# A two-layer streaming encoder trunk: the scale of the attention scores moves into the queries, and the softmax maximum is written negated

## The chip, the cores and the metric

One Trainium2 chip, one of its cores. The metric is the device time of one execution in microseconds (us). Engines are called by the profile's names: PE (TensorE, matmuls; its weight loads are listed apart as PEld), DVE (VectorE), ACT (ScalarE), POOL (GpSimd) and SP (SyncE, which issues most DMAs). L551 means line 551 of the kernel before.

## The reference

Two layers over 512 frames of width 2048, all in float32. Each layer normalises h, projects it through one wide matrix, and feeds the columns to three attention mixers: A (6 heads, low-rank queries and keys, width 128 + 64 rotary), B (5 heads; an indexer picks 128 keys of each query), and C (5 heads, each the difference of two softmaxes over width 64). Every branch has a SiLU gate. An output projection, a residual and a gated per-layer embedding follow. The scale is 192, 128 or 64 to the power -1/2 (A, B, C).

```python
sc = jnp.einsum('bqhd,bkhd->bhqk', qb, k) * scale
pr = masked_softmax(sc, chunk_mask(blk, s)).astype(v.dtype)
return jnp.einsum('bhqk,bkhd->bqhd', pr, v)
...
a1 = masked_softmax(jnp.einsum('bqhd,bkhd->bhqk', qb[..., 0, :], k1) * scale, mask)
a2 = masked_softmax(jnp.einsum('bqhd,bkhd->bhqk', qb[..., 1, :], k2) * scale, mask)
pr = (a1 - lam * a2).astype(v.dtype)
```

## The kernel before

Float32 products are made of three PE matmuls: every operand is split into a rounded part `hi` (by ACT) and a rest `lo` (by DVE), and `mm3` (L361) adds hi·hi, hi·lo and lo·hi in PSUM. Where both parts of a 64-row operand fit on 128 partitions, `stack` (L266) puts hi on one half and lo on the other, and `mm2` needs two matmuls. `split_into` (L260), `stack`, `twice` (L276) and `split` (L286) make these parts.

A layer runs 15 groups of the input projection (192 matmuls each, one of them 96), then 4 groups of `w_o` and 4 of `w_pg`. Each group accumulates four PSUM tiles called `pp`, over 8 chunks of weights (`wr`, split into `wh` and `wl` at L352 to L357). When a group ends, its four `pp` tiles must be read out before the next group can write the same four banks: by ACT at L636 (a copy to `z`), or for gate columns by DVE at L911 (a product with R) and a SiLU by ACT at L912.

The attention runs as a side stream: after every three projection matmuls `pump` (L405) lets the generator `mixers` issue a piece. In order: the six heads of A (heads 0 to 5), the indexer, the five of C (heads 6 to 10), the five of B (heads 11 to 15); a second stream, `choose` (L780), picks the keys for B by 16 rounds of DVE's MAX and MATCH_REPLACE. For each head and each of 4 query blocks, the scores go to a PSUM tile `at`, `causal` masks it (L558), and `soft` (L547) does the softmax: the row's maximum (L550, DVE), its product with -scale (L551, DVE), exp with that bias and with the scale, and its row sum (L552, ACT), and a reciprocal (L553, DVE). The probabilities `e` are normalised, `attend` (L560) transposes them on PE (L568), splits them into `th` and `tl` (L261, L262) and multiplies with v (at L363 to L365, `at<-th,g`). Then ACT copies the head's output away (L828 and L647 for C, L647 else), and the queries and keys of the next head are rotated on DVE (L538 to L541) and split.

At the end of a layer the gated outputs are split once more (`mix`, L934) and are the moving operand of `w_o`; the first four of them lie in tiles called `z`.

The order of instructions on each engine is not the order of the Python code. The program is built under

```python
with tile.TileContext(nc, schedule_with_timeline_sim=True) as tc:
```

so a scheduler at build time arranges the queues by a model of time of its own. Each engine then runs its queue strictly in that order; a removed instruction can therefore shift what stands next to what in all queues.

Of the kernel before, what the change touches and what calls it, by code (L numbers as in the profile page):

```python
# [15 lines left out]
AF = mybir.ActivationFunctionType  # L16
ALU = mybir.AluOpType
AX = mybir.AxisListType
# [10 lines left out]
SC_A = 192 ** -0.5  # L29
SC_B = 128 ** -0.5  # L30
SC_C = 64 ** -0.5
# [167 lines left out]
def trunk(ctx: ExitStack, tc: tile.TileContext, t, out):  # L199
    nc = tc.nc  # L200
    PE, ACT, DVE, POOL = nc.tensor, nc.scalar, nc.vector, nc.gpsimd
# [9 lines left out]
    def f32(ap):  # L211
        return ap.bitcast(F32)

    def slot(dt=F32):
        return big.tile([128, 512], dt, name="g", tag="g")

    def tmp():
        return work.tile([128, 512], F32, name="t", tag="t", bufs=N_TMP)
# [7 lines left out]
    def at():  # L226
        return psum.tile([128, 512], F32, name="at", tag="at")
# [4 lines left out]
    def sm(n=1):  # L232
        return small.tile([128, 4], F32, name="sm", tag="sm", bufs=16)[:, :n]
# [23 lines left out]
    onesf = const.tile([128, 2], F32, name="onesf")  # L257
    DVE.memset(onesf, 1.0)

    def split_into(hi, lo, src):  # L260
        ACT.activation(hi, src, AF.Copy)  # L261
        DVE.tensor_tensor(lo, src, f32(hi), op=ALU.subtract)  # L262

    TOP, LOW = slice(0, 64), slice(64, 128)

    def stack(y):  # L266

        res = []
        for a, b in ((TOP, LOW), (LOW, TOP)):
            o = slot(F32R)  # L270
            ACT.activation(o[a], y[a], AF.Copy)
            DVE.tensor_tensor(o[b], y[a], f32(o[a]), op=ALU.subtract)
            res.append(o)
        return res

# [7 lines left out]
        DVE.tensor_tensor(lo[b], y[a], f32(hi[a]), op=ALU.subtract)  # L283
        return hi, lo

    def split(src):  # L286
        n = src.shape[1]
        hi, lo = slot(F32R)[:, :n], slot(F32R)[:, :n]
        split_into(hi, lo, src)
        return hi, lo  # L290


# [242 lines left out]
    def rope(src, cs, rows=slice(0, 128)):  # L535

        a, b = tmp(), tmp()
        DVE.stream_shuffle(b[rows], src[rows], SWAP)  # L538
        DVE.tensor_tensor(a[rows], src[rows], cs[0][rows], op=ALU.mult)
        DVE.tensor_tensor(b[rows], b[rows], cs[1][rows], op=ALU.mult)  # L540
        DVE.tensor_tensor(a[rows], a[rows], b[rows], op=ALU.add)  # L541
        return a
# [1 line left out]
    BO = [128 * (i * (i + 1) // 2) for i in range(NB)]  # L544
    KO = [0, 512, 896, 1152]

    def soft(ps, n, scale, e):  # L547

        st = sm(4)
        DVE.tensor_reduce(st[:, 0:1], ps[:, :n], op=ALU.max, axis=AX.X)  # L550
        DVE.tensor_scalar(st[:, 1:2], st[:, 0:1], -scale, None, op0=ALU.mult)  # L551
        ACT.activation(e, ps[:, :n], AF.Exp, bias=st[:, 1:2], scale=scale, accum_out=st[:, 2:3])  # L552
        DVE.reciprocal(st[:, 3:4], st[:, 2:3])  # L553
        return st[:, 3:4]

# [33 lines left out]
    for L in range(DEPTH):  # L589
# [5 lines left out]
        tabA = (cosA, sinA)  # L595
        tab = {}
# [14 lines left out]
        raw = {}  # L611
# [73 lines left out]
        def mla():  # L685
            cq, ckv = [], []
            yield ("cq", 2)
            yield from latents("cq", 3, 384, cq)
            yield ("krki", 0)
            yield from shared_keys()  # L690
            yield ("ckv", 1)
            yield from latents("ckv", 2, 256, ckv)
            yield GAP
            kr = keys["r"]
            for j in range(3):
                g = [cc[:, CC_QG + 3 * L + k:CC_QG + 3 * L + k + 1] for k in range(3)]
                w = chunk("w_uq", L, S_UQ, 2 * j, g[:2]) + chunk("w_uq", L, S_UQ, 2 * j + 1, g[2:])
                q = []
                for m in range(3):
                    ps = at()  # L700
                    for k in range(3):
                        mm3(ps, cut(w[k], slice(128 * m, 128 * m + 128)), cq[k], k == 0, k == 2)
                    q.append(split(ps) if m < 2 else stack(rope(ps, tabA)))
                    yield 1.95
                g = [cc[:, CC_KVG + 2 * L + k:CC_KVG + 2 * L + k + 1] for k in range(2)]

                def nope_key(w):
                    ps = at()
                    for k in range(2):
                        mm3(ps, cut(w[k], slice(0, 128)), ckv[k], k == 0, k == 1)  # L710
                    return split(ps)

                w = chunk("w_ukv", L, S_UKV, 2 * j, g)
                kn = nope_key(w)
                yield 1.3
                vp = []
                for b2 in range(2):
                    ps = at()
                    for b in range(2):
                        bs = slice(128 * (2 * b2 + b), 128 * (2 * b2 + b) + 128)  # L720
                        for k in range(2):
                            mm3(ps[:, 256 * b:256 * b + 256], cut(ckv[k], bs), cut(w[k], slice(128, 384)),
                                k == 0, k == 1)
                    vp.append(split(ps))
                    yield 1.3
                for x in range(2):
                    if x:
                        kn = nope_key(chunk("w_ukv", L, S_UKV, 2 * j + 1, g))
                        yield 1.3
                    yield GAP  # L730
                    probs = new_probs()
                    for i in range(NB):
                        n = 128 * (i + 1)
                        ps = at()
                        qs = slice(128 * i, 128 * i + 128)
                        mm3(ps[:, :n], cut(q[x], qs), cut(kn, slice(0, n)), True, False)
                        mm2(ps[:, :n], q[2][x], qs, kr, n, False, True)
                        causal(ps, i)
                        e = probs[:, BO[i]:BO[i] + n]
                        r = soft(ps, n, SC_A, e)  # L740
                        DVE.tensor_scalar(e, e, r, None, op0=ALU.mult)
                        yield 5 * mm_us(n)
                    yield GAP

                    def v(kb, x=x):
                        o = 256 * (kb % 2) + 128 * x
                        return cut(vp[kb // 2], slice(o, o + 128))

                    yield from attend(probs, v)
                    put_out(2 * j + x, attend.po)  # L750


        bias, score = {}, {}
# [48 lines left out]
            return [("kc", x), ("vc" if x < 4 else "v5", 0)]  # L802

        def diff_ready(x):
            q = stack(rope(raw.pop(("qc", x)), tab["c"]))
            y = rope(raw.pop(("kc", x)), tab["c"])
            return q, [twice(y, c) for c in range(2)], None, value_parts("vc", x)

        def diff_probs(x, ops, probs):
            q, k = ops[:2]  # L810
            for i in range(NB):
                n = 128 * (i + 1)
                qs = slice(128 * i, 128 * i + 128)
                e = probs[:, BO[i]:BO[i] + n]
                e2 = tmp()[:, :n]
                rr = []
                for c in range(2):
                    ps = at()
                    mm2(ps[:, :n], q[c], qs, k[c], n, True, True)
                    causal(ps, i)  # L820
                    rr.append(soft(ps, n, SC_C, (e, e2)[c]))
                DVE.tensor_scalar(e2, e2, rr[1], lam_c[:, L:L + 1], op0=ALU.mult, op1=ALU.mult)
                DVE.scalar_tensor_tensor(e, e, rr[0], e2, op0=ALU.mult, op1=ALU.subtract)
                yield 4 * mm_us(n)
# [19 lines left out]
        def dsa_ready(x):  # L844
            if x == 0:
                tab["b"] = table("b", R)
            q = split(rope(raw.pop(("qb", x)), tab["b"]))
            k = split(rope(raw.pop(("kb", x)), tab["b"]))
            return q, k, None, value_parts("vb", x)

        def dsa_probs(x, ops, probs):
            q, k = ops[:2]
            for i in range(NB):
                n = 128 * (i + 1)
                qs = slice(128 * i, 128 * i + 128)
                ps = at()
                mm3(ps[:, :n], cut(q, qs), cut(k, slice(0, n)), True, i == 0)
                if i == 0:
                    causal(ps, i)
                else:  # L860
                    PE.matmul(ps[:, :n], identb, bias[i][:, :n], start=False, stop=True)
                e = probs[:, BO[i]:BO[i] + n]
                r = soft(ps, n, SC_B, e)
                DVE.tensor_scalar(e, e, r, None, op0=ALU.mult)
                yield 3 * mm_us(n) + n * 0.000422

# [118 lines left out]
        for g in range(4):  # L985
# [8 lines left out]
            for m in range(4):  # L994
                k = 4 * g + m
                r = res[m]
# [8 lines left out]
        for g in range(4):  # L1005
# [13 lines left out]
            for m in range(4):  # L1019
                k = 4 * g + m  # L1020
                s, r = sg[m], res[m]
# [13 lines left out]
    ps = [pp() for _ in range(4)]  # L1035
# [23 lines left out]
    for half in range(2):  # L1059
        s = slice(256 * half, 256 * half + 256)  # L1060
        for c in range(8):
# [5 lines left out]
            if half == 0 and c == 1:  # L1067
                ple = []
                for m, y in enumerate(embedding(3)):
                    ple.append(slot())  # L1070
                    ACT.activation(ple[m], y, AF.Copy)
                    r = slot()
# [8 lines left out]
        for m in range(5):  # L1081
            if m == 0:
                y = acc[:, s]
            else:
                r, y = new[11 + m][:, s], sg[m - 1]
# [27 lines left out]
```

## Time and profile before

| | |
|---|---|
| median of 3 runs | 2316.86 us (2314.5 to 2317.55) |
| the profiled execution: time | 2312.61 us |
| its span, first to last instruction | 2310.8 us |
| PE busy | 2276.2 us, 98% of the span |
| DVE busy | 1414.7 us, 61% |
| ACT busy | 1056.2 us, 46% |
| mean granted PE clock | 0.997 |

The span is covered almost completely by one engine. What is left to lose or to win is therefore found in the list of the times when PE stood idle and of what ended each of them, and not in the busy shares of the others. The profiled execution is one of the quicker ones: its time is 4.25 us under the median.

### The profile page before, as it was taken

The numbers are of one execution on the slowest core, as the hardware profiler recorded it, in microseconds if no ns is written. First come the engines' busy times: TensorE is split into PE (matmuls) and PEld (weight loads), VectorE is DVE, ScalarE is ACT, GpSimd is POOL, SyncE is SP. The second block draws the span as 40 slices with busy tenths as digits, with TensorE's granted clock in tenths as the row PEclk, the third lists the DMA queues.
The fourth block names the chain that finished last, engine by engine and source line by source line (L and its number), as shares of the span: only waits on it lengthen the run. The fifth ranks groups of instructions, "written<-read, shape, count | busy, mean of one in ns | idle before, by whom it ended". The sixth has DMA issues, their size and how long they took to land.

```text
span 2310.8 us, 30164 instructions
## 1 busy us (share of the span) xinstructions
PE 2276.2 (98%) x10978; PEld 1912.9 (83%) x10988; DVE 1414.7 (61%) x3071; ACT 1056.2 (46%) x1947; POOL 114.5 (5%) x204
## 2 busy tenths in 40 slices
PE   8999999999999999999999999999999999999997
PEld 7888888888878888888888888888887887888887
DVE  7755569987777643344556555699687765333445
ACT  6444445455555532233435444445564554222444
POOL 0000000000000011000000000000000000110003
PEclk9999999999999999999999999999999999999998
DMA  6233322332324345344332333223232243553334
GB/s 201 72 95 115 112 87 87 110 100 96 96 91 141 124 141 189 121 128 141 123 100 70 99 118 112 83 94 103 91 104 93 86 164 111 177 168 133 100 101 165
DMA packets 95221, 268.34 MB, mean 116 GB/s; under 512 B 10976, under 2 KB 26848, under 8 KB 95072
## 3 DMA queue, kind: packets, MB, share of 16 engines
q1 hardware_dynamic: 81760, 223.41, 30.0%
q0 software_dynamic: 13312, 43.00, 5.3%
q8 instruction: 86, 1.41, 0.3%
q14 instruction: 63, 0.52, 0.1%
HBM read 235.96 MB, written 30.41 MB: 115 GB/s over the span
## 4 chain that ended last, share of the span: by engine, by line
PE 97%; ACT 1%; DVE 1%; issue 1%; DMA 0%; POOL 0%; SPq 0%; POOLq 0%; ACTq 0%; DVEq 0%
PE pp L363 28%; PE pp L365 27%; PE pp L364 27%; PE at L365 3%; PE at L364 3%; PE at L363 3%; PE at L568 1%; PE at L370 1%; PE at L369 1%; PE at L312 0%; PE at L333 0%; ACT wh L356 0%; DMA x<-in_x_dram 0%; ACT g L261 0%; POOL g L1051 0%
## 5 line engine op out<-in xcount | busy, mean ns | idle before, releaser
L363 PE MATMUL pp<-g,wh 128*128 128x512 f32 (+1 forms) x2432 | 938.4, 387 | 15.3 <-ACT g L261 5.9
L364 PE MATMUL pp<-g,wh 128*128 128x512 f32 (+1 forms) x2432 | 937.0, 386 | 0.0
L365 PE MATMUL pp<-g,wl 128*128 128x512 f32 (+1 forms) x2432 | 910.2, 386 | 0.0
L356 ACT ACTIVATE wh<-wr,cc 128x512 fp32r<-128x512 f32 (+3 forms) x522 | 352.2, 683 | 460.7 <-PE pp L364 310.3
L363 PEld LDWEIGHTS pp<-g,wh 128*128 128x128 f32 x2432 | 458.2, 188 | 105.1 <-ACT g L261 5.9
L364 PEld LDWEIGHTS pp<-g,wh 128*128 128x128 f32 x2432 | 457.9, 188 | 87.4
L365 PEld LDWEIGHTS pp<-g,wl 128*128 128x128 f32 x2432 | 456.2, 188 | 87.5
L357 DVE SCALAR_TENSOR_TENSOR wl<-wr,cc,wh 128x512 fp32r<-128x512 f32 (+3 forms) x522 | 360.1, 697 | 268.3 <-ACT wh L356 261.4
L353 DVE TENSOR_TENSOR wl<-wr,wh 128x512 fp32r<-128x512 f32 x288 | 199.5, 697 | 409.8 <-ACT wh L352 375.4
L352 ACT ACTIVATE wh<-wr 128x512 fp32r<-128x512 f32 x288 | 180.3, 630 | 438.9 <-PE pp L364 402.3
L365 PE MATMUL pp<-wh,g 128*128 128x512 f32 (+1 forms) x384 | 136.3, 358 | 0.0
L364 PE MATMUL pp<-wl,g 128*128 128x512 f32 (+1 forms) x384 | 136.1, 358 | 0.0
L363 PE MATMUL pp<-wh,g 128*128 128x512 f32 (+1 forms) x384 | 122.7, 362 | 0.9 <-ACT wh L356 0.8
L552 ACT ACTIVATE e<-at,sm 128x128 f32<-128x128 f32 (+3 forms) x128 | 66.8, 524 | 71.5 <-DVE sm L551 69.4
L365 PEld LDWEIGHTS pp<-wh,g 128*128 128x128 f32 x384 | 72.2, 188 | 9.6
L364 PEld LDWEIGHTS pp<-wl,g 128*128 128x128 f32 x384 | 72.3, 188 | 9.4
L363 PEld LDWEIGHTS pp<-wh,g 128*128 128x128 f32 x384 | 69.9, 188 | 10.7 <-ACT wh L356 1.3
L550 DVE TENSOR_REDUCE sm<-at 128x1 f32<-128x128 f32 (+3 forms) x168 | 77.2, 480 | 1.6
L649 POOL DMA_DIRECT2D o_d<-t x32 | 17.3, 540 | 1134.1 <-ACT t L647 1134.1
L262 DVE TENSOR_TENSOR tl<-at,th 128x512 fp32r<-128x512 f32 (+3 forms) x128 | 54.4, 482 | 28.2 <-ACT th L261 27.8
L261 ACT ACTIVATE th<-at 128x512 fp32r<-128x512 f32 (+3 forms) x128 | 45.6, 439 | 24.3 <-PE at L568 24.3
L568 PE MATMUL at<-identf,e 128*128 128x128 f32 x320 | 55.0, 274 | 0.0
(224 smaller groups left out, 2543.0 us busy)
## 6 DMA issues: line engine op xcount, KB each, us to landing
wr<-in_w_in_dram SPq DMA_DIRECT2D x207, 512.0 KB, 3.6
wr<-in_w_pg_dram SPq DMA_DIRECT2D x72, 512.0 KB, 3.7
wr<-in_w_o_dram SPq DMA_DIRECT2D x64, 512.0 KB, 3.7
o_d<-t POOLq DMA_DIRECT2D x32, 256.0 KB, 2.3
g<-o_d SPq DMA_DIRECT2D x32, 256.0 KB, 4.3
hm_d<-t POOLq DMA_DIRECT2D x32, 256.0 KB, 3.1
wr<-in_w_in_dram SPq DMA_DIRECT2D x18, 256.0 KB, 2.6
wr<-in_w_in_dram SPq DMA_DIRECT2D x16, 264.0 KB, 2.7
```

The source lines that it names most:

```text
L261: ACT.activation(hi, src, AF.Copy)
L262: DVE.tensor_tensor(lo, src, f32(hi), op=ALU.subtract)
L352: ACT.activation(hi, r, AF.Copy)
L353: DVE.tensor_tensor(lo, r, f32(hi), op=ALU.subtract)
L356: ACT.activation(hi, r, AF.Copy, scale=g)
L357: DVE.scalar_tensor_tensor(lo, r, g, f32(hi), op0=ALU.mult, op1=ALU.subtract)
L363: PE.matmul(ps, l[0], r[0], start=start, stop=False)
L364: PE.matmul(ps, l[0], r[1], start=False, stop=False)
L365: PE.matmul(ps, l[1], r[0], start=False, stop=stop)
L550: DVE.tensor_reduce(st[:, 0:1], ps[:, :n], op=ALU.max, axis=AX.X)
L552: ACT.activation(e, ps[:, :n], AF.Exp, bias=st[:, 1:2], scale=scale, accum_out=st[:, 2:3])
L568: PE.transpose(ps[:, 128 * (i - kb):128 * (i - kb) + 128], probs[:, BO[i] + 128 * kb:BO[i] + 128 * kb + 128], identf)
```

## The change

The factor `scale` leaves `soft`. It is applied where the queries are split into parts: ACT writes hi = round(scale · q), and DVE writes lo = scale · q - hi by one instruction with a scalar operand instead of a plain subtraction. `soft` then takes the maximum with `negate=True` straight into the column that the exp reads as its bias; the product with -scale is gone, 168 times in the program.

```diff
-    def split_into(hi, lo, src):
-        ACT.activation(hi, src, AF.Copy)
-        DVE.tensor_tensor(lo, src, f32(hi), op=ALU.subtract)
+    def split_into(hi, lo, src, scale=None):
+        if scale is None:
+            ACT.activation(hi, src, AF.Copy)
+            DVE.tensor_tensor(lo, src, f32(hi), op=ALU.subtract)
+        else:
+            ACT.activation(hi, src, AF.Copy, scale=scale)
+            DVE.scalar_tensor_tensor(lo, src, scale, f32(hi), op0=ALU.mult, op1=ALU.subtract)
...
-    def stack(y):
+    def stack(y, scale=1.0):
...
-            ACT.activation(o[a], y[a], AF.Copy)
-            DVE.tensor_tensor(o[b], y[a], f32(o[a]), op=ALU.subtract)
+            ACT.activation(o[a], y[a], AF.Copy, scale=scale)
+            DVE.scalar_tensor_tensor(o[b], y[a], scale, f32(o[a]), op0=ALU.mult, op1=ALU.subtract)
...
-    def soft(ps, n, scale, e):
+    def soft(ps, n, e):
...
-        DVE.tensor_reduce(st[:, 0:1], ps[:, :n], op=ALU.max, axis=AX.X)
-        DVE.tensor_scalar(st[:, 1:2], st[:, 0:1], -scale, None, op0=ALU.mult)
-        ACT.activation(e, ps[:, :n], AF.Exp, bias=st[:, 1:2], scale=scale, accum_out=st[:, 2:3])
+        DVE.tensor_reduce(st[:, 1:2], ps[:, :n], op=ALU.max, axis=AX.X, negate=True)
+        ACT.activation(e, ps[:, :n], AF.Exp, bias=st[:, 1:2], accum_out=st[:, 2:3])
...
-                    q.append(split(ps) if m < 2 else stack(rope(ps, tabA)))
+                    q.append(split(ps, SC_A) if m < 2 else stack(rope(ps, tabA), SC_A))
...
-            q = stack(rope(raw.pop(("qc", x)), tab["c"]))
+            q = stack(rope(raw.pop(("qc", x)), tab["c"]), SC_C)
...
-            q = split(rope(raw.pop(("qb", x)), tab["b"]))
+            q = split(rope(raw.pop(("qb", x)), tab["b"]), SC_B)
```

PE, ACT, POOL and SP issue as many instructions as before. DVE issues 168 fewer, and 70 of its subtractions (22 at L262, 48 at L272) take the form with a scalar. But the scheduler arranges the queues anew, in most of the stretch in which the heads run, and alike in both layers. Three places matter to the prediction. In the rows the numbers behind the names are those of buffers; line numbers of the kernel after are 1 to 4 higher up to L550 and 3 higher behind it.

Place 1: head 8 (the third of C) ends while the `pp` tiles of the group of qb0, kb0, qb1 and kb1 (5056 to 5059 before, 5000 to 5003 after) are read out. First ACT's queue, before:

```order
L636 ACTIVATE z_5510<-pp_5056 128x512
L636 ACTIVATE z_5512<-pp_5057 128x512
L356 ACTIVATE wh_5675<-wr_5673,cc_75 128x512
L261 ACTIVATE th_4537<-at_4539 128x512
L261 ACTIVATE th_4537<-at_4546 128x384
L261 ACTIVATE th_4537<-at_4552 128x256
L261 ACTIVATE th_4537<-at_4569 128x128
L356 ACTIVATE wh_5679<-wr_5673,cc_75 128x512
L828 ACTIVATE t_4657<-at_4579 128x512
L647 ACTIVATE t_4663<-at_4579 128x512
L261 ACTIVATE g_4659<-t_4657 128x512
L636 ACTIVATE z_5514<-pp_5058 128x512
```

The same stretch of ACT's queue after:

```order
L262 ACTIVATE th_4489<-at_4491 128x512
L262 ACTIVATE th_4489<-at_4498 128x384
L262 ACTIVATE th_4489<-at_4504 128x256
L639 ACTIVATE z_5446<-pp_5000 128x512
L262 ACTIVATE th_4489<-at_4521 128x128
L639 ACTIVATE z_5448<-pp_5001 128x512
L360 ACTIVATE wh_5607<-wr_5605,cc_75 128x512
L360 ACTIVATE wh_5611<-wr_5605,cc_75 128x512
L831 ACTIVATE t_4609<-at_4531 128x512
L650 ACTIVATE t_4615<-at_4531 128x512
L262 ACTIVATE g_4611<-t_4609 128x512
L639 ACTIVATE z_5450<-pp_5002 128x512
```

In both, the third `pp` tile is read out behind the three instructions that wait for the head's output. The first two are read out before the splits of the transposes before, and among them after. PE's queue from the end of the head's product, before:

```order
L365 MATMUL at_4579<-th_4537,g_4427 128x128
L365 MATMUL pp_5518<-g_141,wl_5680 128x512
L365 MATMUL pp_5519<-g_141,wl_5680 128x512
L363 MATMUL pp_5520<-g_123,wh_5524 128x512
L364 MATMUL pp_5520<-g_124,wh_5524 128x512
```

And after; behind the last row shown stand 12 more rows on 5454 and 5455, and then the first on 5456:

```order
L369 MATMUL at_4531<-th_4489,g_4387 128x128
L367 MATMUL pp_5455<-g_123,wh_5460 128x512
L368 MATMUL pp_5455<-g_124,wh_5460 128x512
L369 MATMUL pp_5455<-g_123,wl_5461 128x512
L367 MATMUL pp_5454<-g_127,wh_5464 128x512
L368 MATMUL pp_5454<-g_128,wh_5464 128x512
L369 MATMUL pp_5454<-g_127,wl_5465 128x512
L367 MATMUL pp_5455<-g_127,wh_5464 128x512
L368 MATMUL pp_5455<-g_128,wh_5464 128x512
L369 MATMUL pp_5455<-g_127,wl_5465 128x512
```

Before, two matmuls stand between the head's product and the first that needs the third bank (5520); after, 21 stand there (5456).

Place 2: head 11 (the first of B). PE's queue around the last transpose of its probabilities, before:

```order
L365 MATMUL pp_6472<-g_141,wl_6625 128x512
L363 MATMUL pp_6473<-g_141,wh_6624 128x512
L364 MATMUL pp_6473<-g_142,wh_6624 128x512
L365 MATMUL pp_6473<-g_141,wl_6625 128x512
L568 MATMUL at_5666<-identf_88,e_5575 128x128
L363 MATMUL at_5686<-th_5640,g_5562 128x512
L364 MATMUL at_5686<-tl_5641,g_5562 128x512
```

And after:

```order
L571 MATMUL at_5598<-identf_88,e_5511 128x128
L368 MATMUL pp_6397<-g_138,wh_6540 128x512
L369 MATMUL pp_6397<-g_137,wl_6541 128x512
L367 MATMUL pp_6396<-g_141,wh_6544 128x512
L368 MATMUL pp_6396<-g_142,wh_6544 128x512
L369 MATMUL pp_6396<-g_141,wl_6545 128x512
L367 MATMUL pp_6397<-g_141,wh_6544 128x512
L368 MATMUL pp_6397<-g_142,wh_6544 128x512
L369 MATMUL pp_6397<-g_141,wl_6545 128x512
L367 MATMUL at_5618<-th_5572,g_5498 128x512
```

Eight projection matmuls have moved between the last transpose and the product with v. In both, the next row behind the product's 12 matmuls is the first on a `pp` tile that DVE's L911 must have read out.

Place 3: the end of layer 0, DVE's queue from the third to the fourth `z` rest that `w_o` needs, before:

```order
L262 TENSOR_TENSOR z_7537<-g_5043,z_7536 128x512
L262 TENSOR_TENSOR g_7545<-g_6043,g_7544 128x512
L921 TENSOR_TENSOR g_7501<-g_7501,z_7498 128x512
L262 TENSOR_TENSOR g_7561<-g_6049,g_7560 128x512
L262 TENSOR_TENSOR g_7587<-g_6451,g_7586 128x512
L262 TENSOR_TENSOR z_7541<-g_5049,z_7540 128x512
```

And after:

```order
L263 TENSOR_TENSOR z_7453<-g_4987,z_7452 128x512
L924 TENSOR_TENSOR g_7411<-g_7411,z_7408 128x512
L263 TENSOR_TENSOR g_7561<-g_6799,g_7560 128x512
L924 TENSOR_TENSOR g_7417<-g_7417,z_7414 128x512
L263 TENSOR_TENSOR g_7587<-g_7097,g_7586 128x512
L263 TENSOR_TENSOR g_7603<-g_7109,g_7602 128x512
L263 TENSOR_TENSOR g_7637<-g_7399,g_7636 128x512
L357 TENSOR_TENSOR wl_7537<-wr_7534,wh_7536 128x512
L263 TENSOR_TENSOR g_7653<-g_7405,g_7652 128x512
L357 TENSOR_TENSOR wl_7541<-wr_7534,wh_7540 128x512
L263 TENSOR_TENSOR z_7457<-g_4993,z_7456 128x512
```

Five more instructions stand before the fourth. In layer 1 the queue before reads as layer 0's does after, but for the place of two rows.

## Rows read from the trace of the kernel before

**Rows 1.** The page: busy time of PE and DVE, and the chain of work that ended last, by engine.
```profile
PE 2276.2 (98%) x10978; PEld 1912.9 (83%) x10988; DVE 1414.7 (61%) x3071; ACT 1056.2 (46%) x1947; POOL 114.5 (5%) x204
...
PE 97%; ACT 1%; DVE 1%; issue 1%; DMA 0%; POOL 0%; SPq 0%; POOLq 0%; ACTq 0%; DVEq 0%
```

**Rows 2.** The waits of PE: who waited for whom, us in total, how many times, the longest.
```profile
PE pp L363 <- ACT g L261: 5.9, 1, 5.9
PE pp L363 <- DVE z L911: 4.9, 2, 2.5
PE pp L363 <- ACT z L636: 4.1, 4, 1.7
...
PE at L363 <- DVE tl L262: 1.7, 2, 0.8
...
PE pp L363 <- ACT wh L356: 1.2, 3, 0.4
...
PE at L369 <- ACT g L281: 0.4, 2, 0.2
```

**Rows 3.** The views of lines 551 and 550: durations in ns (shortest, median, longest), and who waited for L551 (us, times).
```profile
L551 DVE TENSOR_SCALAR sm<-sm x168: 122/142/156, 126.3 to 1893.2; 128x1 f32<-128x1 f32 x168
...
  ACT e L552: 69.4, 58
...
L550 DVE TENSOR_REDUCE sm<-at x168: 226/480/693, 125.7 to 1891.7; 128x1 f32<-128x128 f32 x42, 128x1 f32<-128x256 f32 x42, 128x1 f32<-128x384 f32 x42, 128x1 f32<-128x512 f32 x42
```

**Rows 4.** Groups of instructions, shapes kept apart: busy us in total, mean ns of one, idle before. Splits with a scalar (L357, L356) and without (L353, L352).
```profile
L357 DVE SCALAR_TENSOR_TENSOR wl<-wr,cc,wh 128x512 fp32r<-128x512 f32 x416 | 307.4, 745 | 227.1 <-ACT wh L356 223.8 <-PE pp L365 1.9
L353 DVE TENSOR_TENSOR wl<-wr,wh 128x512 fp32r<-128x512 f32 x288 | 199.5, 697 | 409.8 <-ACT wh L352 375.4 <-PE at L364 16.3 <-PE at L365 12.6
...
L356 ACT ACTIVATE wh<-wr,cc 128x512 fp32r<-128x512 f32 x416 | 297.1, 723 | 390.3 <-PE pp L364 286.4 <-PE pp L365 39.1 <-issue 15.1
L352 ACT ACTIVATE wh<-wr 128x512 fp32r<-128x512 f32 x288 | 180.3, 630 | 438.9 <-PE pp L364 402.3 <-PE at L364 31.4 <-issue 2.9
```

**Rows 5.** Instructions of DVE in order of time: start in us, duration in us, instruction.
```profile
464.83 0.12 DVE L551 TENSOR_SCALAR sm<-sm 128x1 f32<-128x1 f32 x1
464.89 0.41 DVE L788 MAX8 top<-g 128x8 f32<-128x256 f32 x1
```

**Rows 6.** Place 1 in order of time: ACT behind the product of head 8, and PE (in brackets the idle time before, and what ended it).
```profile
535.84 0.60 ACT L828 ACTIVATE t<-at 128x512 f32<-128x512 f32 x1 [5.52 <-PE at L365]
...
537.33 0.60 ACT L636 ACTIVATE z<-pp 128x512 f32<-128x512 f32 x1
...
540.71 0.60 ACT L636 ACTIVATE z<-pp 128x512 f32<-128x512 f32 x1
...
537.98 0.50 PE L363 MATMUL pp<-g,wh 128*128 128x512 f32 x1 [1.67 <-ACT z L636]
538.32 0.40 PE L364 MATMUL pp<-g,wh 128*128 128x512 f32 x1
538.55 0.39 PE L365 MATMUL pp<-g,wl 128*128 128x512 f32 x1
...
541.36 0.50 PE L363 MATMUL pp<-g,wh 128*128 128x512 f32 x1 [0.37 <-ACT z L636]
```

**Rows 7.** Place 2 in order of time: PE from the transposes of head 11 on, and DVE behind the last of them.
```profile
640.13 0.87 PE L568 MATMUL at<-identf,e 128*128 128x128 f32 x6
640.76 0.47 PE L363 MATMUL pp<-g,wh 128*128 128x512 f32 x1
...
643.94 0.27 PE L568 MATMUL at<-identf,e 128*128 128x128 f32 x1
643.96 0.47 PE L363 MATMUL at<-th,g 128*128 128x512 f32 x1
...
645.80 0.27 PE L365 MATMUL at<-th,g 128*128 128x128 f32 x1
648.54 0.50 PE L363 MATMUL pp<-g,wh 128*128 128x512 f32 x1 [2.47 <-DVE z L911]
...
647.80 0.68 DVE L911 TENSOR_TENSOR z<-pp,R 128x512 f32<-128x512 f32 x1
```

**Rows 8.** Place 3 in order of time: in layer 1 DVE's second L911 of the last group, its fourth `z` rest and PE's wait for it; in layer 0 the fourth rest, and PE's matmul that needs it.
```profile
1913.64 0.69 DVE L911 TENSOR_TENSOR z<-pp,R 128x512 f32<-128x512 f32 x1 [0.67 <-PE pp L365]
...
1926.88 0.68 DVE L262 TENSOR_TENSOR z<-g,z 128x512 fp32r<-128x512 f32 x1
...
1927.62 0.50 PE L364 MATMUL pp<-z,wh 128*128 128x512 f32 x1 [2.23 <-DVE z L262]
...
782.54 0.68 DVE L262 TENSOR_TENSOR z<-g,z 128x512 fp32r<-128x512 f32 x1
...
785.43 0.39 PE L364 MATMUL pp<-z,wh 128*128 128x512 f32 x1
```

**Rows 9.** The stretch in which DVE is busiest (busy us and number of instructions of each engine, granted clock, DMA), and in it DVE's first L911 and PE's first matmul on the bank that it reads out.
```profile
380.00:480.00 100.00, 100.00 (x458) 83.21 (x457) 97.94 (x272) 49.25 (x89) 0.54 (x1) 1.00 0.33 104
...
472.99 0.67 DVE L911 TENSOR_TENSOR z<-pp,R 128x512 f32<-128x512 f32 x1
...
475.49 1.73 DVE L550 TENSOR_REDUCE sm<-at 128x1 f32<-128x384 f32 x3
...
476.61 0.39 PE L363 MATMUL pp<-g,wh 128*128 128x512 f32 x1
```

More of the change, by code (lines that the diff above doesn't have):

```diff
@@ L284, in twice, with split @@
         return hi, lo
-    def split(src):
+    def split(src, scale=None):
         n = src.shape[1]
         hi, lo = slot(F32R)[:, :n], slot(F32R)[:, :n]
-        split_into(hi, lo, src)
+        split_into(hi, lo, src, scale)
         return hi, lo
@@ L739, in mla @@
                         e = probs[:, BO[i]:BO[i] + n]
-                        r = soft(ps, n, SC_A, e)
+                        r = soft(ps, n, e)
                         DVE.tensor_scalar(e, e, r, None, op0=ALU.mult)
@@ L820, in diff_probs @@
                     causal(ps, i)
-                    rr.append(soft(ps, n, SC_C, (e, e2)[c]))
+                    rr.append(soft(ps, n, (e, e2)[c]))
                 DVE.tensor_scalar(e2, e2, rr[1], lam_c[:, L:L + 1], op0=ALU.mult, op1=ALU.mult)
@@ L862, in dsa_probs @@
                 e = probs[:, BO[i]:BO[i] + n]
-                r = soft(ps, n, SC_B, e)
+                r = soft(ps, n, e)
                 DVE.tensor_scalar(e, e, r, None, op0=ALU.mult)
```

## The prediction

> **What bounds the kernel now.** I read the page first. PE is busy for 98% of the span and the chain that ended last is PE to 97%, while DVE is at 61% [rows 1]. So time can be won only where PE stands idle, and the second view is the list of PE's waits [rows 2]. Without the start (5.9, the wait for ACT's first split) the waits that the attention or the gates cause are: 4.9 us in two waits for DVE's L911, 4.1 us in four for ACT's L636, 1.7 for `tl`, 1.2 for `wh`, 0.4 for the splits of keys at L281, and one of 2.2 for a `z` rest at L262, which stands in rows 8. Together that is 14.5 us, 0.6% of the time. No line of the softmax is among them: L552 waited 69.4 us for L551 [rows 3], but that is ACT waiting, and PE did other work meanwhile. After each wait the first matmul costs about 0.11 us more than its turn, which I add to every one that goes (the pitch of 512-column matmuls is 0.23 us, 538.32 to 538.55 [rows 6]; the first after the wait starts 0.34 before the second).
>
> **The change part by part.** *The removed product.* Each L551 is on record with 142 ns [rows 3], 168 of them being 24 us, but the next instruction starts 0.06 us behind it [rows 5]. In the queue it is worth 168 x 0.06 = 10 us of DVE, and in the chain of one softmax 0.14 us plus the passing on. PE waits for none of this, so by itself it gives nothing.
>
> *The negated maximum.* The trace has no negated reduction. The nearest row is L550 as it is, 480 ns [rows 3]. The bounds are nothing and a second pass, +0.46 to 0.48 us each. I take nothing, since the row is the same operation on the same data; the other end is a rival below.
>
> *The scale in the splits.* For DVE, a subtraction with scalar and column takes 745 ns against 697 without [rows 4]: 70 x 0.05 = 3.4 us. For ACT, a split with a scale from a column takes 723 against 630 [rows 4], and the new one is a constant in the instruction: 0 to 0.09 us each, 0 to 6.5 us in all. These stand ahead of a head's first scores, where PE has only 0.4 us of waits in two places [rows 2], and projection matmuls cover them. I take nothing, with 0.1 us for each of the 32 heads (3 us) as the upper end, if that cover were gone.
>
> *The new order.* The scheduler's order is the part that reaches PE. I take it place by place, alike in both layers where nothing else is said.
>
> Place 1. PE waits 1.67 us for the third `pp` tile and 0.37 for the fourth [rows 6], as ACT reads them out behind the three instructions that wait for the head's product. That product ends at 535.8, when L828 starts; the third tile is out at 537.33 + 0.60 = 537.93, 2.1 us later, and the fourth at 541.31, 5.5 us later [rows 6]. After, 21 projection matmuls instead of 2 stand between the product and the first on the third bank, 21 x 0.23 = 4.8 us, and 33, or 7.5 us, before the first on the fourth. ACT needs about as long as before, since what went ahead of the product (two reads of `pp`, the splits) went into time in which ACT idled for 5.5 us [rows 6]. Both waits go: 1.67 + 0.37 + 2 x 0.11 = 2.26, in both layers **-4.5 us**.
>
> Place 2. The last transpose starts at 643.94, L911 ends at 647.80 + 0.68 = 648.48, 4.5 us later, and PE, whose last matmul of the product started at 645.80, waits 2.47 [rows 7]. L911 stands in DVE's queue behind the splits of these transposes, so it moves with them; eight matmuls put between transpose and product give PE 8 x 0.23 = 1.8 us to do meanwhile. What is late next is the same L911, with some 0.7 us left of the wait: **-3.6 us** for both.
>
> The splits of keys (L281): after, ACT makes them ahead of the gates, and PE comes later than they are ready by an estimated 0.8 us. 0.4 + 2 x 0.11 goes: **-0.6**.
>
> Place 3. In layer 1 PE waits 2.23 for the fourth `z` rest [rows 8]. From the second L911's end, 1914.33, to the rest's start, 1926.88, 21 instructions run, 0.6 us each; one of them goes, -0.6. In layer 0 the rest ends at 783.22 and PE takes it at 785.43, 2.2 us in hand [rows 8]; after, the queue is that of layer 1, the head ends earlier and five more instructions of 0.6 stand ahead of the rest, so that the wait of layer 1 appears there too, 1.6 + 0.1. Net **+1.1**.
>
> Transposes. Six in a row start 0.105 us apart (640.13 to 640.76), but one alone between matmuls of 512 columns costs 0.02 (643.94 to 643.96) [rows 7]. The new order has 18 more that are followed at once by another: 18 x 0.085 = **+1.5**.
>
> The stretch in which DVE is full (98 of 100 us [rows 9]) is where a new wait would come. There DVE's L911 ends at 473.66 and PE needs its bank at 476.61 [rows 9]. The new queue has ahead of it four more maxima (4 x 0.48), three wide instructions (0.6 each), five narrow ones (0.06 each), and twelve L551 (0.06) and one of 0.41 [rows 5] fewer: 1.9 + 1.8 + 0.3 - 0.7 - 0.4 = 2.9 us later, 476.6. PE comes later too, by two matmuls for column sums and four transposes, at an estimated 477.8. The margin of 1.2 us holds; its cost is 0.
>
> The sum is -4.5 - 3.6 - 0.6 + 1.1 + 1.5 = -6.1 us: the profiled execution's 2312.61 becomes 2306.5. It lay 4.25 us under the median shown, and I put the same difference to the median: 2316.86 - 6.1 = 2310.8.
>
> **The rivals.** *No change* (2315 to 2317.5). The arrangement moves waits and removes none: what place 1 gives comes back in small waits at other points, since some 240 blocks of PE's queue stand elsewhere and I have followed only those that waited before. For it: at 98% [rows 1] there is always another thing late by a microsecond, place 3 and the transposes show two; against it: the matmuls put between lie just where PE waited, and elsewhere the margins of before are microseconds. It comes to about 6 us given back, 2316.5.
>
> [...]
>
> *Slower* (about 2323). The negated maximum makes a second pass over its row. Each reduction then takes 0.46 us longer, and in the full stretch [rows 9] 16 of them, of heads 6 and 7, stand ahead of the L911: it comes 7.4 us later, against a margin of 1.2 us, and PE stands 6.2 us in each layer. That is -6.1 + 12.4 = +6.3, 2323. It decides from 1.2 us of lateness there, that is, from 0.08 us for each reduction, so that a smaller price would do too. For it: the trace has no such reduction, and DVE has nothing to spare there; against it: DVE's 98% there hold instructions that start ahead of their need.
>
> [...]
>
> *More gained* (about 2307). Besides the above, the wait at place 3 of layer 0 does not appear (-1.7), and of the 1.7 us for `tl` and 1.2 for `wh` [rows 2] most goes too, since DVE has 10 us less to do: -6.1 - 1.7 - 2.4 = -10. Against it: these waits stand where the order is almost as before, at heads whose queue has few L551.
>
> **How the numbers follow.** The forecast has 0.50; its own range is 2308 to 2313.5, from the terms that rest on order alone (place 3 and the transposes, +2.6 or 0) and the 3 us of the scaled splits. No change has 0.26, more gained 0.12, slower 0.12. This kernel can be told from no change by about 0.2%, 4.6 us, so faster means under 2312.2: 0.43 of the forecast's 0.50 and the 0.12 make 0.55. Within the bound lie 0.07 of the forecast and the 0.26, 0.33; slower keeps 0.12. The range leaves out the slower case and half of the larger gain: 2306 to 2318.
>
> **What would show it.** Right: of PE's waits for L636 nothing is left, of those for L911 under 2 us; two waits for a `z` rest of about 1.7 appear in place of one of 2.2; L550 keeps its 0.48 us. Wrong: a new wait for L911 near 477 (slower), or PE's idle time as long as before under other names (no change). The split of the queries shows at L263 and L276 with at most 0.75 us for DVE.

## The result, and the profile after

The kernel after takes 2302.79 us (median of 6 runs, 2301.65 to 2304.84) where the kernel before takes 2315.65 (6 runs, 2313.85 to 2317.55): ratio 0.9947, 95% interval 0.9936 to 0.9957, or 12.9 us less. The forecast was 2310.8 and the range 2306 to 2318. The direction was right, the gain twice what was forecast, and the time lies below the range.

The profiled execution took 2302.70 us, its span 2300.9. Two lines of its page, the busy times and the chain:

```profile
PE 2274.2 (99%) x10988; PEld 1913.2 (83%) x10988; DVE 1400.3 (61%) x2903; ACT 1053.5 (46%) x1947; POOL 114.5 (5%) x204
...
PE 97%; DVE 1%; issue 1%; ACT 0%; DMA 0%; POOL 0%; SPq 0%; POOLq 0%; DVEq 0%; ACTq 0%
```

DVE has lost 14.4 us of work, PE 2.0 of busy time, and the span 9.9: neither busy time says where that came from. The waits of PE do (us in total, times, longest; L639, L914, L263 and L360 are the lines L636, L911, L262 and L356 of before):

```profile
PE pp L367 <- ACT g L262: 5.7, 1, 5.7
PE pp L368 <- DVE z L263: 3.3, 2, 1.6
PE at L367 <- DVE tl L263: 1.7, 2, 0.9
...
PE pp L367 <- DVE z L914: 1.3, 2, 0.6
...
PE pp L367 <- ACT wh L360: 0.3, 1, 0.3
```

Against [rows 2], the four waits for L636 (4.1 us) and the two for L281 (0.4) are gone, those for L911 have fallen from 4.9 to 1.3, those for `wh` from 1.2 to 0.3, and the one for a `z` rest (2.2) has become two of 1.6. The `tl` waits stay. Of the three `wh` waits before, the two at 226 and 1364 us, 0.42 each, are gone; the one at the start, some 14 us in, is left, and it varies between the traces of either order (0.4 us in that of before and 1.3 with the product kept; 0.3 in that of after and 0.9 in that of the last experiment).

Place 1, ACT in order of time (start, duration, instruction, and in brackets its idle time before); it answers to [rows 6]:

```profile
532.08 0.60 ACT L831 ACTIVATE t<-at 128x512 f32<-128x512 f32 x1 [2.03 <-PE at L369]
...
533.58 0.60 ACT L639 ACTIVATE z<-pp 128x512 f32<-128x512 f32 x1
535.65 1.28 ACT L275 ACTIVATE g<-t 64x512 fp32r<-64x512 f32 x2 [1.47 <-DVE t L545]
536.96 0.60 ACT L639 ACTIVATE z<-pp 128x512 f32<-128x512 f32 x1
```

The third bank is out 2.1 us after the head's product (532.08 to 534.18) and the fourth 5.5 us (537.56), as before and as forecast; PE comes later and waits for neither. What holds the fourth is also to be read here: ACT's split at L275 waits 1.47 us for the rotation on DVE, which stands behind the split of this head's output.

Places 2 and 3, PE (answering to [rows 7, 8]):

```profile
644.20 0.50 PE L367 MATMUL pp<-g,wh 128*128 128x512 f32 x1 [0.64 <-DVE z L914]
...
782.86 0.50 PE L368 MATMUL pp<-z,wh 128*128 128x512 f32 x1 [1.63 <-DVE z L263]
...
1917.59 0.50 PE L368 MATMUL pp<-z,wh 128*128 128x512 f32 x1 [1.63 <-DVE z L263]
```

The stretch in which DVE is full, and the two L914 in it (answering to [rows 9]):

```profile
380.00:480.00 100.00, 100.00 (x464) 83.28 (x464) 99.51 (x265) 47.92 (x93) 0.54 (x1) 1.00 0.33 103
...
475.91 1.27 DVE L914 TENSOR_TENSOR z<-pp,R 128x512 f32<-128x512 f32 x2
```

DVE is busy for 99.5 of 100 us, more than before, since more of the heads' work has moved into this stretch; the first L914 comes 2.9 us later than before, as the sum had it; PE has no gap.

The new and changed instructions: the view of the maximum (shortest, median, longest in ns), then groups by shape (busy us, mean ns of one). The first two groups are the scaled and the plain rest of `at` tiles in the kernel after, the next two the stacked rest after and before, the last two ACT's stacked split after and before.

```profile
L554 DVE TENSOR_REDUCE sm<-at x168: 216/476/693, 126.7 to 1882.7; 128x1 f32<-128x128 f32 x42, 128x1 f32<-128x256 f32 x42, 128x1 f32<-128x384 f32 x42, 128x1 f32<-128x512 f32 x42
```

```profile
L266 DVE SCALAR_TENSOR_TENSOR g<-at,g 128x512 fp32r<-128x512 f32 x12 | 8.3, 690 | 24.5 <-ACT g L265 24.5
...
L263 DVE TENSOR_TENSOR g<-at,g 128x512 fp32r<-128x512 f32 x24 | 16.5, 687 | 11.5 <-ACT g L262 11.5
...
L276 DVE SCALAR_TENSOR_TENSOR g<-t,g 64x512 fp32r<-64x512 f32 x48 | 32.9, 686 | 3.4 <-ACT g L275 2.0
...
L275 ACT ACTIVATE g<-t 64x512 fp32r<-64x512 f32 x48 | 30.2, 628 | 10.3 <-DVE t L545 9.6
```

```profile
L272 DVE TENSOR_TENSOR g<-t,g 64x512 fp32r<-64x512 f32 x48 | 32.9, 686 | 3.4 <-ACT g L271 2.0
...
L271 ACT ACTIVATE g<-t 64x512 fp32r<-64x512 f32 x48 | 30.2, 629 | 11.7 <-DVE t L541 11.1
```

The negated maximum takes 476 ns at the median, the plain one 480 [rows 3]. A scale that is a constant in the instruction costs neither engine anything that can be seen: 686 ns with and without on DVE, 628 and 629 on ACT.

### The profile page after: what moved, and what is told of

Its sections match the earlier page's. It is cut to its first block, busy times and chain, and to the rows that moved or that the text cites. A ratio compares the mean times of both kernels' runs of the same rounds, so it can differ in the third digit from the quotient of the medians.

```text
span 2300.9 us, 30007 instructions
## 1 busy us (share of the span) xinstructions
PE 2274.2 (99%) x10988; PEld 1913.2 (83%) x10988; DVE 1400.3 (61%) x2903; ACT 1053.5 (46%) x1947; POOL 114.5 (5%) x204
## 4 chain that ended last, share of the span: by engine, by line
PE 97%; DVE 1%; issue 1%; ACT 0%; DMA 0%; POOL 0%; SPq 0%; POOLq 0%; DVEq 0%; ACTq 0%
PE pp L367 28%; PE pp L368 28%; PE pp L369 28%; PE at L369 3%; PE at L368 3%; PE at L367 3%; PE at L571 1%; PE at L374 1%; PE at L373 1%; PE at L316 0%; PE at L337 0%; DMA x<-in_x_dram 0%; PE at L864 0%; POOL g L1054 0%; ACT wh L360 0%
## 5 line engine op out<-in xcount | busy, mean ns | idle before, releaser
L360 ACT ACTIVATE wh<-wr,cc 128x512 fp32r<-128x512 f32 (+3 forms) x522 | 351.6, 683 | 473.1 <-PE pp L368 317.3
L357 DVE TENSOR_TENSOR wl<-wr,wh 128x512 fp32r<-128x512 f32 x288 | 199.4, 697 | 412.7 <-ACT wh L356 378.1
L356 ACT ACTIVATE wh<-wr 128x512 fp32r<-128x512 f32 x288 | 180.1, 630 | 442.2 <-PE pp L368 406.8
L263 DVE TENSOR_TENSOR tl<-at,th 128x512 fp32r<-128x512 f32 (+3 forms) x128 | 54.3, 482 | 26.7 <-ACT th L262 26.2
L262 ACT ACTIVATE th<-at 128x512 fp32r<-128x512 f32 (+3 forms) x128 | 45.8, 439 | 20.7 <-PE at L571 20.7
L374 PE MATMUL at<-g 128*128 128x512 f32 (+3 forms) x176 | 53.8, 326 | 0.0
```

The lines of the kernel that those rows point to most:

```text
L356: ACT.activation(hi, r, AF.Copy)
L357: DVE.tensor_tensor(lo, r, f32(hi), op=ALU.subtract)
L360: ACT.activation(hi, r, AF.Copy, scale=g)
L374: PE.matmul(ps, q[:, qs], k[1][:, :n], start=False, stop=stop)
```

## The experiments

Each was timed beside the kernel before on the same chip; ratios are to it, with their 95% intervals. In all but one (the product kept) the order of the queues is held. At the end of the program every instruction of PE, ACT and DVE gets a dependency, without a semaphore, on the one that stands before it in a list:

```python
for eng, text in QUEUES.items():
    order = queue(text)
    ins = [found[eng][k] for k in order]
    for a, b in zip(ins, ins[1:]):
        tc.add_manual_dep(b, a.name, info, reason="order")
```

The lists are read from the built programs of before and after; SP's and POOL's queues come out in the same order by themselves. So the order and the instructions can be exchanged one without the other, and a few rows can be moved alone.

**The instructions of before in the order of after.** The kernel before, with the lists of after, and each product put back behind its maximum:

```diff
 L550 TENSOR_REDUCE sm<-at
+L551 TENSOR_SCALAR sm<-sm
```

> The kernel before, with its 168 products by -scale and its plain subtractions, but with the queues of PE, ACT and DVE held to the order of the kernel after (each product right behind its maximum). Theory, the gain is the order's and the product's time is covered: the profile shows the waits of the kernel after (two for a z rest of 1.6, two for L911 of 0.6, none for L636), and the time is that of the kernel after, about 2303 (ratio 0.9945). Rival, the gain is the work taken off DVE: the time goes back to that of the kernel before, 2312 or more (ratio over 0.998).

It took 2302.47 us (2302.26 to 2303.44), ratio 0.9945 (0.9931 to 0.9958), with DVE busy for 1423.0 us. Its waits:

```profile
PE pp L364 <- DVE z L262: 3.3, 2, 1.6
PE at L363 <- DVE tl L262: 1.7, 2, 0.9
...
PE pp L363 <- DVE z L911: 1.3, 2, 0.6
```

All 168 products are back, and the time is that of the kernel after. The work taken off DVE is worth nothing by itself.

**The instructions of after in the order of before.** The reverse: the kernel after, with the lists of before less the products.

> The kernel after, without the products and with scaled splits, but with the queues of PE, ACT and DVE held to the order of the kernel before. Theory, the gain is the order's: PE's waits are those of the kernel before (1.7 and 0.4 for L636 and 2.5 for L911 in each layer, one z rest of 2.2), and the time is that of the kernel before within 1.5 us, 2314 to 2317 (ratio over 0.999). Rival, the work taken off DVE counts by itself: 2303 to 2308 (ratio under 0.997).

It took 2314.22 us (2312.66 to 2316.33), ratio 0.9996 (0.9987 to 1.0005): no difference that can be measured (the interval runs from 3.0 us less to 1.2 more). Its waits are those of before, but for the `wh` wait at the start and one on a fourth bank: in layer 0 PE's granted clock is 0.81 on average from 536 to 545, around the wait for the third, which is 3.4 us at 0.50 and is taken up below, and so PE came late enough.

```profile
PE pp L367 <- DVE z L914: 4.9, 2, 2.5
PE pp L367 <- ACT z L639: 3.7, 3, 1.7
PE pp L368 <- DVE z L263: 2.2, 1, 2.2
```

With the run above this settles the cause: order of after, -13 us with either set of instructions; order of before, nothing with either.

**The scale moved, the product kept.** Which part of the change makes the new order?

```diff
-        DVE.tensor_reduce(st[:, 1:2], ps[:, :n], op=ALU.max, axis=AX.X, negate=True)
+        DVE.tensor_reduce(st[:, 0:1], ps[:, :n], op=ALU.max, axis=AX.X)
+        DVE.tensor_scalar(st[:, 1:2], st[:, 0:1], -1.0, None, op0=ALU.mult)
```

> The scale is moved to the splits, but the maximum is taken as before and multiplied by -1 in an instruction of its own; the scheduler is free, and its order is that of the kernel before. Theory, splits with a scalar are covered: as before, 2315 within 1.5 us. Rival, they reach PE at the starts of heads: up to 3 us slower. If it is faster by over 3 us, the splits themselves would carry part of the gain.

It took 2314.84 us (2312.58 to 2317.07), ratio 0.9997 (0.9988 to 1.0006). Left free, the scheduler lays PE's queue out as in the kernel before, row for row. The scaled splits neither cost time that can be measured nor change the order; only taking out the 168 products, with the maximum negated in their place, changes it.

**Place 1 alone.** The kernel before, with 13 projection matmuls moved on PE from ahead of and between the head's product to behind it, in both layers:

```diff
-L363 MATMUL pp_5519<-g_127,wh_5528 128x512
...
-L365 MATMUL pp_5519<-g_137,wl_5676 128x512
 L363 MATMUL at_4579<-th_4537,g_4426 128x512
...
 L363 MATMUL at_4579<-th_4537,g_4426 128x384
-L363 MATMUL pp_5518<-g_141,wh_5679 128x512
...
 L365 MATMUL at_4579<-th_4537,g_4427 128x128
+L363 MATMUL pp_5519<-g_127,wh_5528 128x512
...
+L365 MATMUL pp_5519<-g_137,wl_5676 128x512
+L363 MATMUL pp_5518<-g_141,wh_5679 128x512
...
 L365 MATMUL pp_5518<-g_141,wl_5680 128x512
```

> The kernel before with one thing moved, on PE alone: the 12 matmuls of head 8's product with v stand ahead of 13 projection matmuls that stood before or between them, in both layers, so that 15 instead of 2 projection matmuls stand between the product and the first on the third bank. Theory, the waits at place 1 come from ACT's and DVE's queues that wait for that product, and nothing gives them back: both waits go in both layers, with what PE loses behind each of them, -5.2 us (2310.5 where the kernel before has 2315.7, ratio 0.9978). Rival, the time comes back in other waits: within 1.5 us of the kernel before.

It took 2309.59 us (2307.36 to 2312.45), ratio 0.9974 (0.9966 to 0.9983), 6.2 us less. No wait for L636 is left. The others are as before, but for `wh` (1.9 instead of 1.2, the difference being in the wait at the start):

```profile
PE pp L363 <- DVE z L911: 4.9, 2, 2.5
PE pp L364 <- DVE z L262: 2.2, 1, 2.2
```

**What a wait costs beyond its length.** Up to here the medians moved by more than the waits: 12.9 us where the profiles of before and after differ by 9.9. In the profile of the run with the product kept, PE's granted clock (the column behind the five engines) around place 2 reads

```profile
648.00:650.00 2.00, 0.60 (x3) 0.51 (x4) 2.00 (x5) 1.49 (x2) 0.40 (x1) 1.00 0.34 131
650.00:652.00 2.00, 2.00 (x8) 1.58 (x7) 1.90 (x4) 1.43 (x4) 0.00 (x0) 0.67 0.00 0
652.00:654.00 2.00, 2.00 (x6) 1.60 (x5) 2.00 (x4) 0.93 (x2) 0.00 (x0) 0.50 0.03 8
654.00:656.00 2.00, 2.00 (x10) 1.60 (x9) 1.02 (x2) 1.44 (x3) 0.00 (x0) 0.98 0.31 81
```

and PE in order of time

```profile
649.40 0.50 PE L367 MATMUL pp<-g,wh 128*128 128x512 f32 x1 [2.47 <-DVE z L915]
...
650.67 0.62 PE L369 MATMUL pp<-g,wl 128*128 128x512 f32 x1
651.09 0.63 PE L367 MATMUL pp<-g,wh 128*128 128x512 f32 x1
...
654.08 0.40 PE L368 MATMUL pp<-g,wh 128*128 128x512 f32 x1
```

Some 1.3 us behind the wait PE's granted clock falls from 1.00 to 0.50. From 650.67 to 654.08 PE does 8 matmuls in 3.41 us, 0.43 each instead of 0.23: 1.6 us more than 8 x 0.23. The same stands in the profile of before, at place 2 of layer 1:

```profile
1785.00:1787.00 2.00, 0.27 (x1) 0.27 (x2) 2.00 (x4) 1.49 (x2) 0.54 (x1) 1.00 0.34 131
1787.00:1789.00 2.00, 2.00 (x6) 1.57 (x6) 2.00 (x4) 1.43 (x3) 0.00 (x0) 0.54 0.04 8
1789.00:1791.00 2.00, 2.00 (x7) 1.53 (x7) 1.90 (x5) 1.26 (x3) 0.00 (x0) 0.61 0.00 0
1791.00:1793.00 2.00, 2.00 (x11) 1.65 (x10) 1.66 (x4) 1.14 (x2) 0.00 (x0) 1.00 0.09 20
```

The same wait in layer 0 of that execution, also 2.47, had no such stretch behind it. So such a drop of the clock comes in some executions and not in others. The eleven traces hold ten drops behind waits of up to 2.47 us. By the granted clock of the windows each is some 3.4 us at 0.50, which is eight matmuls at 0.43; in the four whose start can be read (this one, 1787.16 in the profile of before, and two more with the product kept, near 1790.7 and 1930.7) it begins 0.4 to 1.5 us behind the end of the wait. To see whether it makes up the rest, one run shortens the waits and three lengthen them.

**Place 2 alone.** The kernel before, with DVE's two read-outs moved up, in both layers:

```diff
 L539 TENSOR_TENSOR t_5746<-z_5514,cos_5535 128x512
+L911 TENSOR_TENSOR z_6448<-pp_6058,R_107 128x512
 L538 STREAM_SHUFFLE t_5757<-z_5516 128x512
 L539 TENSOR_TENSOR t_5756<-z_5516,cos_5535 128x512
 L540 TENSOR_TENSOR t_5747<-t_5747,sin_5536 128x512
-L911 TENSOR_TENSOR z_6448<-pp_6058,R_107 128x512
+L911 TENSOR_TENSOR z_6460<-pp_6059,R_107 128x512
 L540 TENSOR_TENSOR t_5757<-t_5757,sin_5536 128x512
-L911 TENSOR_TENSOR z_6460<-pp_6059,R_107 128x512
```

> The kernel before with one thing moved, on DVE alone: at place 2 the two L911 stand three and one instructions earlier, in both layers, so that PE's wait of 2.47 becomes about 0.65, as in the kernel after. If the wait costs its length alone: 2 x 1.8 = -3.6 us against the kernel before (ratio 0.9984). [...]

It took 2310.13 us (2309.30 to 2312.14), ratio 0.9981 (0.9972 to 0.9990), 4.7 us less. The two waits came to 1.6 us together instead of 4.9, which is 3.3 us; PE keeps 1.00 near 650 and 1790 (the drops of this execution stand behind a wait of 1.67 at 538 and one of 2.2 at 1924). If the drops behind these waits had gone too, at the rate of 6 in 8 such waits and 1.55 us each that the other traces show, it would be another 2.3 us on the 3.6 expected of their length, 5.9 together, as an estimate. The result lies between the two, and its interval (2.3 to 6.5 us) takes in both. The mean granted clock, which is on record for every run, speaks against the second: it averages 0.9962 in these 11 runs and 0.9961 in the 15 of before beside them (0.9957 in all 63 runs of before beside the experiments), and one drop, 3.41 us at half the clock, takes 0.0007 off it. So, as an estimate, 0.1 to 0.7 drops of an execution went, not 1.5; by that estimate more drops come behind the waits that are kept (two of the three from 1.67 to 2.2 us in this run's profile). At an equal clock of 0.996 these runs take 2310.2 us on average (7 runs), those of before beside them 2314.6 (8 runs): most of the gain isn't fewer drops, and about 1 us of it beyond the 3.3 is not assigned.

**Longer waits.** The kernel after, its order held, with maxima that nobody reads ahead of the read-out at place 2 in both layers (4, 10 and 18 of them):

```diff
+            if len(calls) == 7:
+                for _ in range(10):
+                    DVE.tensor_reduce(junk, identf, op=ALU.max, axis=AX.X)
             s = raw_slot()
             DVE.tensor_tensor(s, z[kind, x], R, op=ALU.mult)
```

> The kernel after in its own order with 4 short maxima over 128 columns, whose results nobody reads, ahead of DVE's read-out of the third bank at place 2, in both layers, so that PE's wait there (0.64) grows by some 0.7 to 1.3. If a wait costs its length alone: +1.3 us against the kernel after. [...]

> The same with 10 maxima: PE's wait at place 2 becomes about 2.3. If a wait costs its length alone: +3.3 us against the kernel after, and its runs agree as closely as those (within some 1.5 us). [...]

> The same with 18 maxima: PE's wait at place 2 becomes about 3.6. Length alone: +6 us against the kernel after. With the lower clock behind the waits: +6 to +9, and the profile shows stretches of a granted clock of 0.5 right behind one or both of them.

| maxima | each of the two waits | longer by, both | time (lowest to highest) | against after | ratio |
|---|---|---|---|---|---|
| 0 (after) | 0.64 | | 2302.79 (2301.65 to 2304.84) | | 0.9947 |
| 4 | 1.8 | 2.3 | 2306.46 (2305.70 to 2308.80) | 3.7 | 0.9966 (0.9952 to 0.9980) |
| 10 | 3.7 | 6.1 | 2313.09 (2311.61 to 2314.09) | 10.3 | 0.9991 (0.9982 to 0.9999) |
| 18 | 6.3 | 11.3 | 2318.20 (2317.21 to 2318.84) | 15.4 | 1.0011 (1.0002 to 1.0020) |

A maximum held DVE for 0.31 us, twice what I had taken, so the waits are longer than the expectations say; I compare with the waits that came. The two longer pairs cost 4.1 to 4.2 us more than their length by the medians, 2 us for each wait; the intervals of the ratios leave some 3 us on either side, and the kernel before took 0.8 us less beside these runs than beside the kernel after. In the profile with 10 maxima the wait ends at 646.30, and the clock is

```profile
646.00:648.00 2.00, 1.70 (x4) 1.41 (x5) 2.00 (x5) 1.15 (x2) 0.00 (x0) 0.50 0.00 0
648.00:650.00 2.00, 2.00 (x6) 1.52 (x6) 1.91 (x5) 1.83 (x4) 0.00 (x0) 0.50 0.00 0
650.00:652.00 2.00, 2.00 (x8) 1.59 (x7) 1.24 (x3) 0.00 (x0) 0.00 (x0) 0.66 0.03 8
```

that is, 0.50 already when the wait ends, for twelve matmuls (646.30 to 651.50, 2.3 us lost). In layer 1 the clock averages 0.93 from 1750 to 1800, some 7 us at 0.50. With 18 maxima it averages 0.96 from 600 to 650 and 0.97 from 650 to 700, and again 0.93 from 1750 to 1800: some 7 us at 0.50 in each layer. With 4 maxima the profile shows no such stretch, and two of the five runs lie 2 us above the others; their mean granted clock is 0.995, that of the other three 0.996 and 0.997. So PE lost 1.6 us behind one wait of 2.47 (the eight matmuls above) and 2.3 behind one of 3.72 (the twelve here).

**A version that beats both.** If only PE's waits are left, the two kinds that the kernel after kept can be moved away. Its DVE queue, place 2 as in the run above, and place 3 (with `z_7456` on ACT three rows earlier), in both layers:

```diff
 L924 TENSOR_TENSOR g_7411<-g_7411,z_7408 128x512
+L924 TENSOR_TENSOR g_7417<-g_7417,z_7414 128x512
 L263 TENSOR_TENSOR g_7561<-g_6799,g_7560 128x512
-L924 TENSOR_TENSOR g_7417<-g_7417,z_7414 128x512
...
 L263 TENSOR_TENSOR g_7637<-g_7399,g_7636 128x512
+L263 TENSOR_TENSOR z_7457<-g_4993,z_7456 128x512
 L357 TENSOR_TENSOR wl_7537<-wr_7534,wh_7536 128x512
 L263 TENSOR_TENSOR g_7653<-g_7405,g_7652 128x512
 L357 TENSOR_TENSOR wl_7541<-wr_7534,wh_7540 128x512
-L263 TENSOR_TENSOR z_7457<-g_4993,z_7456 128x512
```

> The kernel after with a few rows of DVE's and ACT's queues moved, PE's queue as it is: at place 2 DVE reads out the third and fourth bank two and one instructions earlier, at place 3 the fourth z rest and what it needs stand three to four instructions earlier; in both layers. Theory, only PE's waits are left to win: the two waits for L911 (0.64 each, with what PE loses behind them 0.9) and the two for a z rest (1.6 each, 1.9) go, -5.6 us against the kernel after, about 2297 (ratio to before 0.992). Rival, what is moved behind them makes new waits: 2301 or more.

It took 2297.06 us (2296.24 to 2297.30), ratio 0.9921 (0.9909 to 0.9934): 5.7 us under the median of the kernel after, whose interval (0.9936 to 0.9957) lies above this one. No wait of PE for L914 or a `z` rest is left; the longest behind the start are

```profile
PE at L367 <- DVE tl L263: 1.7, 2, 0.9
PE at L337 <- DVE rcolF L331: 1.6, 1, 1.6
```

## Why the prediction came out half the size

What the profiles show of each term of the sum (both layers, us):

| term | forecast | shown |
|---|---|---|
| the removed product by itself | 0 | 0 (order of before without it: 0.9996) |
| the negated maximum | 0 | 0 (476 ns against 480) |
| the scaled splits | 0 | 0 (0.9997) |
| place 1 | -4.5 | -4.1 in its waits, all gone; a like move alone -6.2 in the median |
| place 2 | -3.6 | -3.6 in its waits (4.9 to 1.3); a like move alone -4.7 in the median |
| splits of keys | -0.6 | -0.4, both waits gone |
| place 3 | +1.1 | +1.0 in its waits (2.2 to 3.3) |
| transposes | +1.5 | +1.4, an estimate (17 more in a row in the records, at the forecast's 0.08 each) |
| full stretch | 0 | 0 (the read-out ends at 476.58; forecast 476.6) |
| `wh` at 226 and 1364 | 0 | -0.85 (two of 0.42, both gone) |

But for `wh`, the places, the signs and the length of the waits were right. These two `wh` waits are the order's as well: they stand in all five traces with the order of before and in none of the six with that of after. In the order of after seven transposes in a row stand on PE ahead of the matmul that waited (225.84), where four stood before (225.21), and they run until the split is all but done; the forecast had counted such rows only as a cost.

Two statements were wrong, and they are one error.

First, "After each wait the first matmul costs about 0.11 us more than its turn": that was all I charged to a wait beyond its length. Behind a wait the clock can fall: in the traces with the waits of before it was at 0.50 for some 3.4 us each time, which costs 1.5 to 1.6 us. In the eleven traces (nine of experiments, before and after) such a stretch followed 6 of 8 waits of 2.47 us, 2 of 5 of 2.2, 2 of 8 of 1.67 at place 1, none of 10 of 1.63 at place 3, none of 2 of 1.8, and all 4 of the longer ones. (The last 11.7 us of the trace of before and 13.9 of that of after, where PE has almost nothing to do, are at 0.50 too; such ends are not counted.) The kernel before has five waits of these kinds, the kernel after only the two of 1.63.

Second, "I put the same difference to the median". The profiled execution of before had one drop of the clock, 1.5 us; without it, 2311.1. The median of before, 2315.65, lies 4.5 us over that, while the profiled execution of after, with no drop, agrees with its median (2302.70 and 2302.79). So the difference was not an offset that both kernels share: it went with the waits. By the counts above before has 2 x 2/8 + 2/5 + 2 x 6/8 = 2.4 drops in an execution, an estimate of 3.8 us. Then -12.9 comes out as 2302.7 - 2311.1 = -8.4 for waits and order and some -4 for the clock, of which I had forecast -6.1 and nothing. Of the -8.4 the terms of the table make some -7 (-4.1 and 4 x 0.11 at place 1, -3.6, -0.4, +1.0, +1.4, -0.85); the remaining 1.4 I have not assigned.

That the drops make up the last 4 us is borne out by the runs without a profile. The 63 runs of before beside the experiments have a mean granted clock of 0.9957 on average, the profiled execution with its one drop 0.9967 in its trace; at 0.0007 a drop that is 1.4 more, 2.4 in all, as counted. And their time follows the clock: 2313.5 us on average at 0.997 (8 runs), 2314.5 at 0.996 (29), 2316.6 at 0.995 (23) and 2317.5 at 0.994 (3). Of the six runs of after five are at 0.997, and the slowest, 2304.84, is at 0.996. That the two ways agree on 2.4 is in part luck: the rates by kind of wait did not hold when place 2 was moved alone.

Of the rivals, no change fell: the waits did not come back under other names, neither in the kernel after nor where one place was moved alone. That the work taken off DVE gives nothing by itself held (ratio 0.9996 with the order held), and the gain came by the order. The slower rival fell with the 476 ns: a second pass was to add 0.46 us, and the negated maximum takes no longer than the plain one (480). Of the larger gain (10 us), two of the `wh` waits came true, by the order and not by DVE's lighter load, but the `tl` waits stayed and the wait of layer 0 at place 3 appeared, as forecast. Its size was nearer; its reasons did not hold. The scaled rest of the queries stands at L266 and L276, not at L263 as the prediction has it, and takes 686 to 690 ns, within its bound.

## What to carry to other kernels

Where a scheduler lays out the queues, removing an instruction is two changes, the instruction and the order: hold the order and exchange the instructions before you credit either. Here the 168 instructions were worth nothing that could be measured and the order 13 us, and moving a few rows by hand gave 5.7 us more. For a PE-bound kernel, list its longest waits (here drops came behind waits of 1.67 us and more), and look at the granted clock in windows of 2 us behind each: a profiled execution that is quicker than the median of the runs may be one that had fewer drops (here one, against an estimated 2.4), and the mean granted clock of each run tells (here 2313.5 us on average at 0.997, 2317.5 at 0.994).

## What was not expected of the hardware

PE's granted clock fell from 1.00 to 0.50 behind single waits of 1.67 to 2.47 us in the midst of a program in which it is busy for 98%, for some 3.4 us or eight matmuls (1.6 us lost), in some executions and not in others, at the same instruction. With waits of 3.7 and 6.3 us it did so in both layers of the one execution of each that was profiled. With the 3.7 in layer 0 the clock was down before the wait ended at 646.30: it averages 0.82 from 642 to 646, which puts the fall some 2.0 us into the wait, as an estimate (0.18 x 4 / 0.5 = 1.44 us at 0.50 by 646).

What stays open: why the same wait is followed by a drop in one execution and not in the next, why the drops hardly grew fewer when only place 2 was shortened, and the 1 to 1.4 us that are not assigned.
